# Weight sums for short product units, made stages ahead and kept in DRAM

## The chip, the core and the metric

The kernel runs on one core of one Trainium2 chip, as one program. The core has five engines with queues of their own: PE (TensorE, matmul), DVE (VectorE), ACT (ScalarE), POOL (GpSimd) and SP (SyncE, here only an issuer of DMAs). The metric is the device time of one execution in microseconds, lower is better; a run takes several executions and their median counts.

## What is computed

A trunk of two residual layers over 256 tokens of width 2048, all in float32. Each layer has a token mixer (layer 0: neighbourhood attention with 16 heads; layer 1: a gated short convolution) and a gated MLP of width 5632 with a convolution of three taps between up-projection and activation. Cut to what matters:

```python
for i in range(DEPTH):                       # DEPTH = 2
    a = rms_norm(h, mix_norm[i])
    h = h + (neighborhood_attention(a, ...) if i == 0 else short_conv_mixer(a, ...))
    a = rms_norm(h, ffn_norm[i])
    g, u = jnp.split(dwconv_centered(a @ w_up[i], conv_w) + conv_b, 2, axis=-1)
    h = h + (silu(g) * u) @ w_down[i]
return rms_norm(h, final_norm)
```

## The kernel before

**Precision.** Every float32 operand is split in two parts: `hi`, a copy rounded to the matmul's type (ACT), and `lo = raw - hi` (DVE). A product is the sum of three matmuls, hi x hi, hi x lo and lo x hi. Weights are split on the chip each time they are loaded: `prep_to` takes the next entry of a long list `chunks`, loads up to 512 KB into a buffer tagged `raw` (five of them, from SP's queue, L120 or L124) and calls `parts` (L131), which makes the cast on ACT (L139) and the subtraction on DVE (L140) into buffers `hi` and `lo`, six of each.

**Order.** All stages append their work to three lists: `chunks` (weights to load), `items` (pieces of matmul work) and `ends` (how many chunks an item needs). One loop at the end (L790) goes over the items: it prepares the chunks that the item needs, runs the item, then prepares `AHEAD` = 4 chunks more. `after(n, fn)` puts work off by n ticks of this loop. Each engine runs its own instructions in order; waits are set by the framework from what an instruction reads and writes, and a buffer is taken again only when its last reader is done.

**Two kinds of stage.** A `Phase` (query/key, short convolution "SC", up-projection) has the weights as the stationary operand: for each 128 output columns 16 matmuls of 512 columns (L185) and 16 of 256 (L193), two such columns side by side; each result then goes through an evacuation on ACT and DVE (`both`, `conv`, `split` and others). `Values` (attention's value projection) and `Tokens` (attention's output, the mixer's output, the down-projections) have the tokens as the stationary operand and stream the weights, with the matmuls of `product` (L374). A down-projection comes in two halves of 22 K tiles, each after its own half of the up-projection, which leaves its results in 22 tiles tagged `act`.

**Seven products instead of eight.** `Tokens` works on units: two K tiles, both halves of the tokens, and two groups of 512 columns, a 2 x 2 by 2 x 2 block product. A plain unit takes eight products. The units listed in a plan's second entry go through `seven` (L379): a Winograd form with seven products, which needs sums of the four token blocks (`make_forms`, L421, on POOL, split again on ACT and DVE) and sums of the weight blocks. The weight sums are made by `sums` (L143) when the unit's right-hand chunk arrives: four additions on DVE over 128 x 512, then `parts` for three blocks, of 512, 1024 and 1024 columns. Four of the seven products add up in PSUM tiles of their own (`mu`), and after a plan's last such unit `combine` (L405) adds them to `h`.

**Plans.** Each plan has the order of the units for one pair of column groups, the units in short form, and when `combine` is due. In attention's output the short units are 6 and 7, in the mixer's output 1, 3, 5, in the down-projection's first half 1, 3, 5, 7, 9 in both plans, in the second half 1, 3, 5, 7 and 3, 5, 7. The very last four K tiles of the run are done by `finale` (L364), one output block after the other, so that the closing norm can start early.

**Stages in order of time**: four times query/key and values with attention; attention's output; layer 0: up, down, up, down; SC; mixer's output; layer 1: up, down, up, down, closing norm (`last_evac`).

## Time and profile before

| what | value |
|---|---|
| median of 3 runs | 2204.95 us (2203.89 to 2205.58) |
| span of the profiled execution | 2203.5 us |
| DVE busy | 1752.7 us (80%) |
| ACT busy | 1274.6 us (58%) |
| DMA: moved, mean rate | 421.00 MB, 191 GB/s |
| DMA queue of SP, share of the 16 DMA engines | 58.4% |
| DMA queue of ACT | 0.63 MB |
| written to HBM | 2.10 MB |
| granted clock of PE | 0.998 |

The page gives for each engine the time in which it was busy, and its share of the span. The span runs from the first to the last instruction; the time of a run is a little longer than the span, and the profiled execution's own run isn't among the three. Tables by stage give, after the stretch and its length, the busy time of each engine with its number of instructions, then the granted clock, the share of the DMA engines and the rate. A row of a group of instructions has the line in the code, the engine, the operation, what it writes and reads, how often it ran, the total and the mean in ns, and the idle time before it with what ended that. "A <- B: t, n, longest" in a list of waits says that A waited t us for B, n times.

### The profile page before, as it was taken

Reading aid. Unit: us, or ns where it says so; the run is one execution under the profiler, and the core shown is the slowest. Engines: PE = TensorE matmul, PEld = TensorE weight load, DVE = VectorE, ACT = ScalarE, POOL = GpSimd, SP = SyncE. Lnnn points to the kernel's source line nnn. Section 1 sums busy time; section 2 is a strip of 40 time slices with the busy share of each in tenths; the row PEclk is TensorE's granted clock in tenths of the full one; section 3 lists DMA queues with packets and bytes.
Section 4 is the critical chain, followed back from the end, with each engine's and each line's share of the span. In section 5 each row is a group of like instructions: output and inputs, shape, how many; then the busy total and the mean of one; then the engine's idle time right before and its main releaser. Section 6 shows DMA issues by size and latency. Waiting matters only on the chain.

```text
span 2203.5 us, 31950 instructions
## 1 busy us (share of the span) xinstructions
PE 2191.7 (99%) x11776; PEld 1900.1 (86%) x11776; DVE 1752.7 (80%) x2677; ACT 1274.6 (58%) x1900; POOL 71.4 (3%) x115
## 2 busy tenths in 40 slices
PE   9999999999999999999999999999999999999998
PEld 8888888888888888888888888888888888888886
DVE  8777678877788987778876666898777898777887
ACT  7555556665655565565555445566556556665554
POOL 0000000000000000000000000000000000000000
PEclk9999999999999999999999999999999999999999
DMA  7565546555556755555665555565555566555564
GB/s 259 191 198 180 172 150 211 190 191 191 191 172 196 226 200 186 191 190 185 200 196 189 187 191 183 174 224 180 190 187 184 177 212 219 191 191 192 170 203 134
DMA packets 214605, 421.00 MB, mean 191 GB/s; under 512 B 13488, under 2 KB 142640, under 8 KB 214448
## 3 DMA queue, kind: packets, MB, share of 16 engines
q1 hardware_dynamic: 213072, 418.33, 58.4%
q8 instruction: 92, 1.51, 0.3%
q10 hardware_dynamic: 1376, 0.63, 0.1%
q14 instruction: 65, 0.53, 0.1%
HBM read 416.81 MB, written 2.10 MB: 190 GB/s over the span
## 4 chain that ended last, share of the span: by engine, by line
PE 96%; DVE 1%; DMA 1%; ACT 1%; issue 0%; SPq 0%; DVEq 0%; ACTq 0%
PE mm L185 41%; PE mm L193 22%; PE mm L375 8%; PE mm L376 8%; PE mm L377 8%; PE mu L375 2%; PE mu L377 2%; PE mu L376 2%; PE mm L570 1%; PE mm L572 1%; PE mm L571 1%; DMA raw<-in_wqk 1%; PE tr L284 1%; DVE lo L140 0%; PE tr L525 0%
## 5 line engine op out<-in xcount | busy, mean ns | idle before, releaser
L140 DVE TENSOR_TENSOR lo<-raw,hi 128x1024 fp32r<-128x1024 f32 (+1 forms) x836 | 973.1, 1186 | 188.3 <-PE mm L193 123.4
L139 ACT CAST hi<-raw 128x1024 fp32r<-128x1024 f32 (+1 forms) x836 | 845.7, 1019 | 368.9 <-PE mm L377 121.8
L185 PE MATMUL mm<-a,hi 128*128 128x512 f32 x4096 | 961.7, 391 | 0.9 <-ACT hi L139 0.4
L185 PEld LDWEIGHTS mm<-a,hi 128*128 128x128 f32 x4096 | 759.2, 188 | 153.8 <-DVE a L226 2.0
L193 PEld LDWEIGHTS mm<-a,lo 128*128 128x128 f32 x4096 | 512.9, 192 | 11.9
L193 PE MATMUL mm<-a,lo 128*128 128x256 f32 x4096 | 518.0, 283 | 0.0
L375 PE MATMUL mm<-hi,act 128*128 128x512 f32 x696 | 271.4, 390 | 0.0
L376 PE MATMUL mm<-lo,act 128*128 128x512 f32 x696 | 271.1, 389 | 0.0
L377 PE MATMUL mm<-hi,act 128*128 128x512 f32 x696 | 270.8, 389 | 0.0
L238 ACT COPY corr<-mm 128x256 f32<-128x256 f32 x256 | 94.8, 372 | 240.0 <-PE mm L193 240.0
L254 DVE SCALAR_TENSOR_TENSOR conv<-pad,pt,conv 128x256 f32<-128x256 f32 x384 | 184.8, 482 | 43.8 <-ACT conv L252 28.8
L252 ACT ACTIVATE conv<-pad,pt 128x256 f32<-128x256 f32 x176 | 105.6, 601 | 145.8 <-DVE pad L244 145.8
L377 PEld LDWEIGHTS mm<-hi,act 128*128 128x128 f32 x696 | 130.6, 188 | 27.2
L375 PEld LDWEIGHTS mm<-hi,act 128*128 128x128 f32 x696 | 130.7, 188 | 26.8
L376 PEld LDWEIGHTS mm<-lo,act 128*128 128x128 f32 x696 | 130.7, 188 | 26.6
L239 DVE TENSOR_TENSOR corr<-mm,corr 128x256 f32<-128x256 f32 x256 | 106.9, 418 | 2.0 <-ACT corr L238 1.9
L218 DVE TENSOR_TENSOR act<-conv,act 128x256 fp32r<-128x256 f32 x88 | 37.4, 425 | 85.8 <-ACT act L217 85.8
L244 DVE TENSOR_TENSOR pad<-corr,rstd 128x256 f32<-128x256 f32 x176 | 74.0, 421 | 0.1
L139 ACT CAST hi<-t 128x1024 fp32r<-128x1024 f32 x44 | 46.4, 1054 | 39.6 <-DVE t L152 26.5
L140 DVE TENSOR_TENSOR lo<-t,hi 128x1024 fp32r<-128x1024 f32 x44 | 53.8, 1222 | 4.8 <-ACT hi L139 3.7
L149 DVE TENSOR_TENSOR raw<-raw 128x512 f32<-128x512 f32 x44 | 30.4, 690 | 33.2 <-DMA raw<-in_wdown 28.9
L570 PE MATMUL mm<-hi,a 128*128 128x512 f32 x128 | 50.5, 394 | 0.0
(157 smaller groups left out, 1464.0 us busy)
## 6 DMA issues: line engine op xcount, KB each, us to landing
raw<-in_wup SPq DMA_DIRECT2D x352, 512.0 KB, 4.9
raw<-in_wdown SPq DMA_DIRECT2D x176, 512.0 KB, 4.5
raw<-in_wsc SPq DMA_DIRECT2D x96, 512.0 KB, 4.9
raw<-in_wqk SPq DMA_DIRECT2D x56, 512.0 KB, 4.7
raw<-in_wv SPq DMA_DIRECT2D x32, 512.0 KB, 4.5
raw<-in_wo SPq DMA_DIRECT2D x32, 512.0 KB, 4.5
raw<-in_wscout SPq DMA_DIRECT2D x32, 512.0 KB, 4.4
raw<-in_wqk SPq DMA_DIRECT2D x16, 256.0 KB, 5.1
```

The costliest lines, as they stand in the source:

```text
L139: nc.scalar.copy(out=hv, in_=r)
L140: nc.vector.tensor_sub(out=lv, in0=r, in1=hv.bitcast(F32))
L185: nc.tensor.matmul(self.ps[ft], lhsT=prepped[i][0][:, o:o + P], rhs=self.src[k], start=k == 0, stop=False)
L193: nc.tensor.matmul(self.ps[ft][:, S:], lhsT=prepped[i][1][:, o:o + P], rhs=self.src[k][:, :S], start=False, stop=k == self.nk - 1)
L238: nc.scalar.copy(out=corr, in_=ps[:, S:])
L239: nc.vector.tensor_add(out=corr, in0=ps[:, :S], in1=corr)
L244: nc.vector.tensor_mul(out=dst, in0=both(ps), in1=rstd)
L252: nc.scalar.activation(c, x[:, 1:S + 1], AF.Identity, scale=w[1], bias=b)
L254: nc.vector.scalar_tensor_tensor(out=c, in0=x[:, tap:tap + S], scalar=w[tap], in1=c, op0=ALU.mult, op1=ALU.add)
L375: nc.tensor.matmul(ps, lhsT=xh, rhs=wh, start=start, stop=False)
L376: nc.tensor.matmul(ps, lhsT=xh, rhs=wl, start=False, stop=False)
L377: nc.tensor.matmul(ps, lhsT=xl, rhs=wh, start=False, stop=stop)
```

## The change

It has five parts.

1. **More short units.** Plans are written as words: P plain, S short with sums made on arrival as before, D short with sums made earlier. Each of the four plans of a down-projection's two halves has six short units, two S and four D; the mixer's output has one S and three D in each plan, attention's output keeps its two S.
2. **Jobs.** Each D unit is made in two jobs of kind "make", which stand in `chunks` between the weights of `Phase` stages. A job loads two 256 KB pieces from SP's queue into two `act` tiles, adds four times on DVE (128 x 256 each, four chunks later in the list), and stores the two tiles from ACT's queue into a DRAM tile (seven chunks later). 16 jobs stand in the second and third query/key stages, 8, 8, 8 and the last 2 in the four up-projections, 34 in SC, between an eighth and three quarters of a stage's items (from the first item where that eighth is less than one item).
3. **Loading a D unit.** Four chunks: the left block (512 KB), the second K tile of the right one (256 KB) and two kept ones (512 KB each). `seven` takes the sums in the arrangement in which they were kept, and for a D unit does product "21" two places earlier.
4. **Room.** `sums` makes its second pair in the right-hand chunk's own buffer, not in a tile tagged `qk`. A set of token forms takes 6 blocks of a tile instead of 8; the fourth form goes into the part of an `act` tile that a short unit doesn't read, with a split of its own. `corr` has two buffers instead of four (every other one of the first query/key results goes to a tile tagged `g`). The 512-column blocks of the right chunk share one buffer for `hi` and `lo`.
5. **A sixth `raw` buffer.**

```diff
+S_FIRST = (plan("P0 D1 P2 S3 D4 P5 D6 S7 P8 D9 P10", 3), plan("P0 P2 D1 S3 D4 P5 D6 S7 P8 P10 D9", 6))
+S_SECOND = (plan("P0 P2 D1 S3 D4 P5 D6 S7 D8 P9 P10", 1), plan("P0 P2 P5 D1 S3 D4 S7 D6 D8 P9 P10", 1))
+S_OUT = (plan("P0 D1 S2 P3 D4 D5 P6 P7", 1), plan("P0 P3 D1 S2 D4 D5 P6 P7", 1))
+QK_JOBS, UP_JOBS, SC_JOBS = (0, 8, 8, 0), (8, 8, 8, 4), 34
+S_ATT = (plan("P0 P1 P2 S6 P3 S7 P4 P5", 1),) * 2
...
+RAWS = 6
...
     def prep_to(n):
         while len(prepped) < min(n, len(chunks)):
             src, w, kind = chunks[len(prepped)]
-            raw = wp.tile([P, CH * P], F32, name="raw", tag="raw", bufs=5)
+            for due in [x for x in stores if x[0] <= len(prepped)]:
+                stores.remove(due)
+                due[1]()
+            if kind == "make":
+                make(src, w)
+                prepped.append(())
+                continue
+            raw = wp.tile([P, CH * P], F32, name="raw", tag="raw", bufs=RAWS)
...
+            if kind == "kept":
+                nc.sync.dma_start(out=raw, in_=src().rearrange("p h n -> p (h n)"))
...
     def sums(l, r):
...
         add(out=v13[:, :, 1, :], in0=r[:, :, 1, :], in1=r[:, :, 0, :])
-        add(out=v24[:, :, 0, :], in0=v13[:, :, 0, :], in1=r[:, :, 1, :])
-        add(out=v24[:, :, 1, :], in0=v24[:, :, 0, :], in1=l[:, :, 1, :])
-        return parts(r[:, :, 1:2, :]), parts(t13), parts(t24)
+        w22 = parts(r[:, :, 1:2, :])
+        add(out=r[:, :, 1, :], in0=v13[:, :, 0, :], in1=r[:, :, 1, :])
+        add(out=r[:, :, 0, :], in0=r[:, :, 1, :], in1=l[:, :, 1, :])
+        return w22, parts(t13), parts(r)
+
+    def make(job, half):
+        w, g, i = job
+        if half == 0:
+            kept[id(w), g, i] = dp.tile([P, 2, 2, 4 * P], F32, name=f"kept{len(kept)}")
+        dst = kept[id(w), g, i]
+        tiles = [act_tile().bitcast(F32) for _ in range(2)]
+        for n, x in enumerate(tiles):
+            f = 8 * g + 4 * n + 2 * half
+            nc.sync.dma_start(out=x.rearrange("p (f n) -> p f n", f=2),
+                              in_=w[f:f + 2, :, 2 * i * P:(2 * i + 2) * P].rearrange("f p n -> p f n"))
+        l, r = (x.rearrange("p (f k c) -> p k f c", f=2, k=2) for x in tiles)
+
+        def adds():
+            add = nc.vector.tensor_add
+            add(out=l[:, 0], in0=l[:, 0], in1=r[:, 0])
+            add(out=r[:, 0], in0=r[:, 1], in1=r[:, 0])
+            add(out=r[:, 1], in0=l[:, 0], in1=r[:, 1])
+            add(out=l[:, 1], in0=r[:, 1], in1=l[:, 1])
+
+        def store():
+            for n, x in enumerate(tiles):
+                nc.scalar.dma_start(out=dst[:, n, half], in_=x)
+        stores.append((len(prepped) + 4, adds))
+        stores.append((len(prepped) + 7, store))
...
+            made, lo, hi = 0, len(order) // 8, len(order) * 3 // 4
+            for n, (two, ks) in enumerate(order):
...
                 ends.append(len(chunks))
+                while made < min(len(jobs), max(0, -(-len(jobs) * (n + 1 - lo) // (hi - lo)))):
+                    chunks.append((*jobs[made], "make"))
+                    made += 1
...
+                    elif i in kinds:
+                        chunks.append((right[:, :, P:], P, "cols"))
+                        chunks.extend((lambda j=j, key=(id(w), g, i): kept[key][:, j], 2 * P, "kept") for j in range(2))
+                        items.append((self, g, c + 1, k, k, k + 2))
+                        ends.append(c + 4)
...
-            for ps, x, w, j in ((a, raw(0, 0), left, 0), ("11", raw(1, 0), left, 1), ("12", s4, w22, 0),
-                                (e, s1, t13, 0), (f, s3, t13, 1), (b, s2, t24, 0), ("21", raw(1, 1), t24, 1)):
+            if sset[i] == "S":
+                w22, (t1, t3), (t4, t2) = prepped[c][0], *([(y, j) for j in range(2)] for y in prepped[c][1:])
+            else:
+                w22, (t1, t4), (t3, t2) = prepped[c], *([(y, j) for j in range(2)] for y in prepped[c + 1:c + 3])
+            for ps, x, (w, j) in ((a, raw(0, 0), (left, 0)), ("11", raw(1, 0), (left, 1)), ("12", s4, (w22, 0)),
+                                  (e, s1, t1), *((("21", raw(1, 1), t4),) * (sset[i] == "D")), (f, s3, t3), (b, s2, t2),
+                                  *((("21", raw(1, 1), t4),) * (sset[i] == "S"))):
...
+        n = form_at[0] = (form_at[0] + 1) % 6
+        y = tp.tile([P, 6 * P], F32R, name="sf", tag=("sf", "vv", "qk")[n % 3])
+        hi, lo = y[:, :3 * P], y[:, 3 * P:]
+        split_into(hi, lo, v[:, :3].rearrange("p f c -> p (f c)"))
+        spare = place[:, P:2 * P], place[:, 3 * P:]
+        split_into(*spare, v[:, 3])
```

More of the change, by code (lines that the diff above doesn't have):

```diff
@@ L113, in trunk @@
     prepped = []
+    stores = []
     def prep_to(n):
@@ L312, in __init__ @@
             self.halves = halves
-            for g, (order, sset, _) in enumerate(plan):
+            for g, (order, kinds, _) in enumerate(plan):
                 for i in order:
@@ L467, in qk_evac @@
     def qk_evac(f, ps):
-        c = both(ps)
+        c = both(ps, "g" if waiting and len(held) % 2 else "corr")
         if waiting:
@@ L737, in trunk @@
     mlp(0, a1, to_norm(2, a2))
-    Phase(wsc, range(3 * KT), KT, a2, sc_evac, intro=3)
-    Tokens(wscout, KT, yT, to_norm(3, a3), ((range(KT // 2), S_OUT, 1),) * 2, yforms)
+    Phase(wsc, range(3 * KT), KT, a2, sc_evac, intro=3, jobs=take(SC_JOBS))
+    Tokens(wscout, KT, yT, to_norm(3, a3), S_OUT, yforms)
     mlp(1, a3, last_evac())
```

97 lines of the change are left out of this document (59 added, 38 removed).

## The prediction

> **What bounds the kernel now.** I read the page's busy times first, then the waits of PE and of the load queue, the chain, and last the windows by stage (cut where the timeline's matmuls change from L185/L193 to L375-L377).
>
> ```profile
> PE 2191.7 (99%) x11776; PEld 1900.1 (86%) x11776; DVE 1752.7 (80%) x2677; ACT 1274.6 (58%) x1900; POOL 71.4 (3%) x115
> ...
> PE bc L686 <- DVE conv L684: 1.6, 1, 1.6
> PE st L100 <- DVE inv L645: 1.1, 1, 1.1
> ...
> SPq L120 <- DVE lo L140: 1208.3, 512, 8.2
> SPq L124 <- DVE lo L140: 497.0, 198, 12.6
> ...
> 419.71 7.28 PE mm L185 x32
> 427.00 3.83 PE mm L193 x32
> ```
>
> A busy PE need not be a PE at its peak, so the first line alone proves little. The waits prove it: PE's longest is 1.6 us. The load queue sits 1208.3 and 497.0 us behind VectorE's low-part subtraction (L140), which frees load buffers: loads wait for buffers, not PE for loads. In the chain the matmuls stand back to back, 32 of 512 columns in 7.28 us, 0.2275 us each (32 of 256 columns take 3.83 us). PE sets the end in every stage. What takes matmuls away shortens the run as long as nothing else becomes late.
>
> **The change part by part. Matmuls removed.** A unit (two K tiles, 256 tokens, 1024 columns) has eight products, or seven in the short form, each of three 512-column matmuls. Short units before, from the plans: 5+5+4+3 per MLP layer, 3+3 in the mixer's output, 2+2 in attention's, together 44. After: four plans of 6 per layer, 4+4 and 2+2, together 60. Sixteen more, one product less each: 16 x 3 x 0.2275 = **10.9 us of PE time gone**. No matmul is added.
>
> **Sums moved out of the token stages.** 38 of the 60 are "D" units; two jobs each, 76, make their sums earlier. A job loads 2 x 256 KB, makes four 128x256 additions on VectorE and stores 2 x 256 KB from ACT's queue, 1.05 MB in all. The token stage then loads 512 + 256 + 1024 KB, 1.84 MB instead of 1.05.
>
> ```profile
> L140 DVE TENSOR_TENSOR lo<-raw,hi 128x1024 fp32r<-128x1024 f32 x776 | 935.5, 1224 | 184.4 <-PE mm L193 123.4 <-ACT hi L139 52.2 <-issue 5.8
> L140 DVE TENSOR_TENSOR lo<-raw,hi 128x512 fp32r<-128x512 f32 x60 | 41.0, 688 | 3.9 <-ACT hi L139 3.8
> L151 DVE TENSOR_TENSOR t<-raw 128x512 f32<-128x512 f32 x44 | 30.1, 685 | 0.0
> L601 DVE TENSOR_TENSOR pad<-scx 128x256 f32<-128x256 f32 x16 | 6.8, 423 | 0.2
> ...
> 641.80:754.70 112.90, 112.90 (x500) 93.49 (x499) 101.49 (x124) 64.10 (x70) 0.00 (x0) 1.00 0.67 207
> ```
>
> VectorE in a token stage: an in-place ("S") unit costs 4 x 0.685 + 3 x 1.224 + 0.688 = 7.1 us, a D unit 4.36, a plain one 2 x 1.224 = 2.45. The first down-projection (last row) had 10 S and 12 plain, 100 us by this sum against 101.5 measured; with 4 S, 8 D, 10 plain it is 88, some 89 of 111.5 us. VectorE is relieved there. ACT casts 3.5 blocks of 1024 for a short unit and 2 for a plain one, so it gets three blocks more beside 64.1 of 112.9. The transfers grow from 207 GB/s x 112.9 us = 23.4 MB by 8 x 0.79 to 29.7 MB, 266 GB/s. Value taken: nothing.
>
> **The jobs, where they land.** Eight in each of the second and third query/key stages, 26 in the four up-projections, 34 in the short-convolution (SC) stage, spread from an eighth to three quarters of its items (in the query/key stages from the first). Here covers run thin. An SC item of one chunk is 8 x (0.2275 + 0.12) = 2.78 us, so the 34 fall between the 4th and the 21st of 29 items, from 1124.2 to 1293.7 us.
>
> ```profile
> 83.60:121.60 38.00, 38.00 (x233) 34.11 (x232) 24.45 (x41) 21.12 (x36) 1.02 (x1) 1.00 0.49 154
> 776.90:932.40 155.50, 155.50 (x898) 137.72 (x897) 121.83 (x200) 93.33 (x143) 6.83 (x13) 1.00 0.56 190
> 1124.20:1293.70 169.50, 169.50 (x970) 149.33 (x969) 113.83 (x184) 87.54 (x120) 5.55 (x8) 1.00 0.56 187
> 1115.90:1132.60 16.70, 16.70 (x99) 14.37 (x98) 12.95 (x25) 11.47 (x21) 0.00 (x0) 1.00 0.69 221
> 1132.60:1138.20 5.60, 5.60 (x33) 4.85 (x32) 5.60 (x11) 3.83 (x6) 0.00 (x0) 1.00 0.51 162
> ...
> 690.00:695.00 5.00, 5.00 (x24) 4.14 (x23) 3.68 (x4) 3.10 (x3) 0.00 (x0) 1.00 1.08 380
> 1040.00:1050.00 10.00, 10.00 (x46) 8.26 (x45) 9.45 (x11) 6.82 (x7) 0.00 (x0) 1.00 1.04 353
> ...
> L120 SPq DMA_DIRECT2D raw<-in_wsc x96: 327/328/341, 1097.4 to 1361.6; - x96
> ```
>
> After the times stand PE, PEld, DVE, ACT, POOL, the clock, the DMA share and GB/s.
>
> *VectorE.* A job is 4 x 0.423 = 1.69 us. SC: 113.8 + 34 x 1.69 = 171 us of work in 169.5. Up-projection: 121.8 + 13.5 = 135 of 155.5. Query/key: 24.5 + 13.5 = 38 of 38. SC is worst at its front: four short items (14 us) bring eight jobs, 13.5 us, where VectorE already works 12.95 of 16.7 and 5.60 of 5.6. It falls some 10 us behind and regains under 1 us per pair of columns. A pair's low parts are first read after its 32 high matmuls (7.28 us), and two pairs fit in PSUM, so roughly 10 us of lateness is covered. Bounds: 0 (all covered) to 5 us (the front's overhang counted once and half again). I take **+2 us**, near the covered end, since the front overruns its cover by little.
>
> *DMA.* SC needs 187 GB/s x 169.5 = 31.7 MB plus 34 x 1.05 = 35.7, less some six last stores that slip past the window (3.1): 64.2 MB, or 379 GB/s. Before shows 380 over 5 us and 353 over 10 us, at shares above 1. At 353 it takes 182 us, 12 too many; but the first SC load issues at 1097.4, 18.5 us before its stage, and this lead swallows 12. At 380 nothing is late. I take 0 by the 10 us row, the longer one. Query/key: 154 x 38 = 5.9 + 8.4 = 14.3 MB, 40 us at 353 where there are 38: covered.
>
> A rule of the Trainium skill speaks against this change: the page "DMA: Bandwidth & Descriptors", section "Issuing engines are not separate DMA queues", says that transfers started from SP and from ACT run on the same 16 engines and interleave. By it the stores on ACT's queue count in full, as I counted them; if they ran beside the loads, SC would need only 64.2 - 14.7 = 49.5 MB, 292 GB/s, and no DMA rival were left. No row here has bulk stores.
>
> *Queue order.* A job's load waits on SP for two free activation tiles, with the next weights behind it. 22 exist; each job holds two from its load to its store's landing. A store waits on ACT for VectorE's additions, with the casts behind it; it stands three chunks after them, so it should find them done.
>
> ```profile
> 0.73 0.41 ACTq L94 DMA_DIRECT2D pt<-in_par  x1
> out<-a ACTq DMA_DIRECT2D x4, 128.0 KB, 2.3
> L217 ACT CAST sf<-s 128x512 fp32r<-128x512 f32 x21 | 13.0, 621 | 14.8 <-POOL s L431 14.6
> L218 DVE TENSOR_TENSOR sf<-s,sf 128x512 fp32r<-128x512 f32 x21 | 14.5, 693 | 22.8 <-ACT sf L217 22.8
> ```
>
> Issuing a store costs ACT 0.41 us: 68 in SC, 28 us beside 87.5 of 169.5, hidden. Landing (2.3 us for 128 KB) waits on nobody but the next job.
>
> *Forms.* Token forms grow from 23 to 30 sets, the fourth form now split by itself: 7 more sets of 0.62 us on ACT and 0.69 on VectorE, and one short operation more on each for 28 sets, none longer than those: at most some 5 us of either engine per up-projection half, hidden in the slack above.
>
> *Sixth load buffer, start.*
>
> ```profile
> 0.00:83.60 83.60, 80.62 (x446) 69.91 (x447) 69.46 (x126) 57.42 (x128) 8.62 (x13) 1.00 0.76 251
> ```
>
> PE idles 3.0 us in the first 83.6. A sixth buffer can save between -0.5 and 1.5 of it; I take 0, as later stages wait for buffers from the far side.
>
> *The end.* The last short unit used to be followed by a plain unit before the closing block; now (D8) none stands between.
>
> ```profile
> 2172.55 0.69 DVE L411 TENSOR_TENSOR h<-h,s 128x512 f32<-128x512 f32 x1
> 2180.16 0.69 DVE L417 TENSOR_TENSOR h<-h,s 128x512 f32<-128x512 f32 x1
> 2180.40:2193.50 13.10, 13.02 (x63) 9.87 (x61) 8.30 (x26) 6.29 (x17) 0.00 (x0) 1.00 0.11 34
> 2193.46 0.69 DVE L273 TENSOR_TENSOR h<-mm,h 128x512 f32<-128x512 f32 x1 [0.75 <-PE mm L377]
> ```
>
> The combining additions L410-L417 (eight, 0.6 us apart, about 5 us) stood ahead of the closing block; now they fall into it, on top of VectorE's 8.3 us of 13.1. That fits, barely, before the last residual add. Bounds 0 to 3 us; I take **+1**.
>
> **Sum.** 2203.5 (span) - 10.9 + 2 + 1 = 2195.6. The three runs lie 0.4 to 2.1 us above the span, their median 1.45: **2197.0**.
>
> **Rivals.** (1) *Slower: bulk stores and loads together run below what loads alone reach.* The SC window covers 169.5 + 18.5 (lead) us at no loss; PE then starves for 64.2 MB / rate - 188. The gain of some 10 us is used up at 64.2 / 198 = 324 GB/s. At 300 GB/s the loss is 26 us: 2204.95 - 10.9 + 1 + 26 = 2221. For it: no row shows stores. Against it: share 1.0 went with 353 and 380 GB/s. Chance 0.16. (2) *No change: queues and VectorE give the gain back.* In the query/key stages eight jobs want 16 tiles where eight hold probabilities and four to eight hold outputs: SP may wait up to half a stage (25 us against 18.5 of lead, some 6 each), and SC's front may cost 5 instead of 2. Loss 5 to 14 in place of 2: 2200 to 2209. For it: VectorE at 38 of 38 and 171 of 169.5. Against it: after both backlogs comes a stretch without jobs, and PE's own cover is spent only once. Chance 0.19. (3) *The change doesn't shorten PE's part,* because matmuls next to a fuller SBUF run slower: 1% would cost 22 us. At 380 GB/s above, PE was busy all 5 us; I give it under 0.01 and count it with (1).
>
> **How the numbers follow.** Forecast: 0.62, 2192.5 (no losses, start gains 1.5) to 2200.5. Better than that: 0.03. A measurement here tells about 0.2%, 4.4 us, from no change. Faster by more (below 2200.5): 0.65; within: rival (2), 0.19; slower: rival (1), 0.16. The range of 8 in 10 takes the forecast and rival (2): 2192.5 to 2211.
>
> **What would show it.** Right: 2700 instead of 2748 product matmuls at the same 0.2275 us; token stages about 1.4 to 3.4 us shorter per MLP half (two, then five units) and 1.4 in the mixer's output; SC still near 269 us with DVE near 0.95 and over 350 GB/s. Rival (1): PE waiting for ACT's casts behind late loads in SC, DMA share at 1 with fewer GB/s. Rival (2): SP waiting on stores or on L542's tiles, PE waiting in query/key. Wrong altogether: PE idle in the down-projections.

## The result, and the profile after

The changed kernel takes 2234.0 us (median of 4 runs, 2229.19 to 2236.13) against 2205.22 us for the kernel before on the same chip: ratio 1.013, interval 1.0116 to 1.0145. It is 1.3% slower, where the forecast was 2197.0 us and its range ended at 2211. The profiled execution spans 2231.6 us (before 2203.5, forecast 2195.6).

The page's first part, its shares of the chain and three of its rows for transfers:

```profile
PE 2194.1 (98%) x11728; PEld 1893.3 (85%) x11728; DVE 1836.9 (82%) x2960; ACT 1298.0 (58%) x1967; POOL 102.4 (5%) x143
...
PE 80%; DMA 9%; DVE 7%; issue 2%; ACT 1%; SPq 0%; ACTq 0%; POOL 0%; DVEq 0%
...
raw<-in_wup SPq DMA_DIRECT2D x352, 512.0 KB, 5.0
...
kept<-act ACTq DMA_DIRECT2D x152, 256.0 KB, 4.8
...
act<-in_wdown SPq DMA_DIRECT2D x128, 256.0 KB, 6.0
```

PE ran 48 matmuls fewer, as the change meant, and was yet busy 2.4 us longer and idle 37.5 us in all instead of 11.8. A part of the longer busy time is the clock: right after two of PE's long idle stretches (3.35 us at 1089.4 and 2.45 us at 1452.6) the granted clock was 0.50 for 3.4 us (1093.0 to 1096.4 and 1454.8 to 1458.2), which by that clock is an estimated 1.7 us lost each time; in the kernel before, it fell only at the very end, from 2196.7 us on. The chain that ended last is 9% DMA. The last two rows are the jobs' own: their loads land in 6.0 us (median), their stores in 4.8; above them stand the weight loads of the up-projections.

Stage by stage (windows; after each length stand the busy times of PE, PEld, DVE, ACT, POOL, then clock, DMA share and GB/s): the second query/key stage and its values, the second down-projection of layer 0, SC and the mixer's output of before; then the same of after, and with them the first down-projection of layer 0, whose row of before stands in the prediction.

```profile
83.60:134.50 50.90, 50.90 (x312) 45.74 (x311) 35.09 (x61) 28.96 (x51) 2.04 (x2) 1.00 0.52 165
134.50:157.90 23.40, 23.40 (x113) 19.48 (x112) 17.89 (x29) 11.80 (x22) 2.03 (x2) 1.00 0.71 223
...
999.20:1115.90 116.70, 116.70 (x525) 96.86 (x524) 98.33 (x123) 66.92 (x84) 0.00 (x0) 1.00 0.65 203
1115.90:1385.20 269.30, 269.30 (x1555) 238.14 (x1554) 185.25 (x291) 137.85 (x191) 7.59 (x12) 1.00 0.56 186
1385.20:1470.20 85.00, 85.00 (x385) 70.36 (x384) 78.49 (x102) 51.69 (x69) 0.00 (x0) 1.00 0.63 204
```

```profile
81.80:135.10 53.30, 51.37 (x311) 45.80 (x310) 38.53 (x81) 25.07 (x45) 5.50 (x2) 1.00 0.80 270
135.10:162.50 27.40, 24.28 (x112) 19.55 (x111) 23.59 (x40) 15.08 (x28) 5.85 (x2) 1.00 0.82 273
...
652.30:763.80 111.50, 111.50 (x494) 92.34 (x493) 92.51 (x107) 66.80 (x74) 0.00 (x0) 1.00 0.77 251
1008.30:1132.30 124.00, 117.18 (x511) 94.67 (x509) 106.47 (x139) 72.96 (x91) 0.00 (x0) 0.99 0.82 272
1132.30:1410.20 277.90, 272.39 (x1554) 238.94 (x1555) 223.33 (x413) 135.29 (x200) 15.62 (x16) 1.00 0.88 294
1410.20:1499.40 89.20, 86.28 (x378) 69.82 (x377) 79.28 (x102) 54.21 (x72) 0.00 (x0) 0.98 0.79 268
```

PE fills every stage of before to the last tenth. After, it still does so in the first down-projection, which is 1.4 us shorter (two units x 3 x 0.2275 us), but not in the others shown. All stages of after that aren't in the table below kept their length within 0.2 us. Lengths here and below are from stage cuts as in the prediction, in us; "2nd and 3rd QK+V" are the two query/key stages that have jobs, with their values.

| stage | before | forecast | after | no_jobs | no_adds | no_stores | in_order | spread | best_tied |
|---|---|---|---|---|---|---|---|---|---|
| up to the 2nd QK | 83.6 | 83.6 | 81.8 | 82.1 | 82.7 | 82.2 | 82.5 | 81.9 | 82.0 |
| 2nd and 3rd QK+V | 148.1 | 148.1 | 160.6 | 148.1 | 163.9 | 155.4 | 159.6 | 148.1 | 148.1 |
| layer 0, 1st down | 112.9 | 111.5 | 111.5 | 111.5 | 111.5 | 111.5 | 111.5 | 111.5 | 112.9 |
| layer 0, 2nd down | 116.7 | 113.3 | 124.0 | 116.8 | 125.1 | 119.7 | 116.8 | 115.6 | 116.5 |
| SC | 269.3 | 271.3 | 278.0 | 269.3 | 269.4 | 281.7 | 286.6 | 269.3 | 269.0 |
| mixer's output | 85.0 | 83.6 | 89.2 | 83.6 | 88.0 | 86.4 | 84.0 | 83.6 | 85.0 |
| layer 1, 1st down | 112.9 | 111.5 | 111.5 | 111.5 | 111.5 | 111.5 | 111.5 | 111.5 | 111.5 |
| layer 1, 2nd down | 129.0 | 126.6 | 129.3 | 129.9 | 129.9 | 130.5 | 129.7 | 126.4 | 127.0 |
| span | 2203.5 | 2195.6 | 2231.6 | 2198.9 | 2227.9 | 2224.7 | 2229.1 | 2194.0 | 2198.2 |

The spans of the changed kernel's four runs lie between 2227.4 and 2234.3 us, and the table has one trace of each kernel. So a difference of a few us between two losing stages may be the spread between runs; stages at PE's pace repeat within some 0.4 us.

Against the forecast the span lost 36.0 us: 12.5 in the query/key stages, 10.7 in layer 0's second down-projection, 6.7 in SC, 5.6 in the mixer's output, 2.7 in the last stage, less some 2 won elsewhere, 1.8 of it at the start.

**The wait that the forecast's sum didn't hold.** VectorE's waits for jobs' loads, and PE's two longest waits, after ("A <- B: us in total, times, longest"):

```profile
DVE act L204 <- DMA act<-in_wdown: 34.2, 19, 5.6
...
DVE act L204 <- DMA act<-in_wscout: 11.4, 4, 5.6
```

```profile
PE mu L455 <- DVE lo L172: 5.7, 6, 3.4
PE mm L267 <- DVE lo L172: 5.3, 9, 1.9
```

L204 is a job's first addition. VectorE stood 45.6 us before it because the job's load hadn't landed; the subtractions (L172) queued behind it then kept PE waiting. Here is one place in SC where VectorE stood, from VectorE's timeline (start, length, what, and in brackets the idle time before it):

```profile
1179.65 0.43 DVE L204 TENSOR_TENSOR act<-act 128x256 f32<-128x256 f32 x1 [5.60 <-DMA act<-in_wscout]
1179.99 1.22 DVE L172 TENSOR_TENSOR lo<-raw,hi 128x1024 fp32r<-128x1024 f32 x1
```

Behind this one PE waited only 0.55 us for a subtraction (at 1189.89); behind a stand of 3.31 us before 1277.60 it waited 1.87 us.

Over the whole of SC VectorE's waits for jobs' loads come to 24.3 us (the list of waits, cut to that stage):

```profile
DVE act L204 <- DMA act<-in_wdown: 17.9, 7, 5.6
DVE act L204 <- DMA act<-in_wscout: 6.4, 2, 5.6
```

The loss doesn't come at SC's front, where the prediction looked for it. These are its first 129.7 us and the next 60 us (columns as above):

```profile
1132.30:1262.00 129.70, 129.15 (x742) 114.06 (x743) 106.44 (x209) 63.96 (x98) 6.67 (x8) 1.00 0.93 308
1262.00:1322.00 60.00, 55.04 (x306) 46.84 (x305) 47.26 (x90) 24.05 (x35) 1.65 (x1) 1.00 0.96 334
```

In the first stretch VectorE stood 14.7 us for loads and PE was idle for 0.55 us; in the second it stood 9.0 us more and PE was idle for 4.96 us. In in_order (below), with all 34 jobs in SC, PE was busy for the whole of SC's first 70 us. So the cover for VectorE's lateness seems to have lasted for the 18 jobs of the first stretch and to have been used up then.

And one place in the second query/key stage, from the chain (start, length, what) and from ACT's timeline:

```profile
124.90 7.97 DMA act<-in_wdown
...
132.96 0.42 DVE act L204
133.39 0.34 DVE act L206
133.72 1.16 DVE act L205
```

```profile
129.87 0.40 ACT L291 CAST qk<-qk 128x256 fp32r<-128x256 f32 x1
133.76 2.31 ACTq L211 DMA_DIRECT2D kept<-act  x3
136.11 0.37 ACT L312 COPY corr<-mm 128x256 f32<-128x256 f32 x1 [5.84 <-DMA kept<-act]
```

The job's load took 7.97 us to land, the additions came at once behind it, and ACT did nothing from 130.27 to 133.76 because the next thing in its queue was a store that waited for an addition. Three stores then took 2.31 us to issue, and an evacuation (L312) came after 5.84 us without work on ACT. The bracket names the store's transfer; what held ACT is the store standing ahead of the copy, which the ACTq row between them shows. The Trainium skill, page "DMA: Bandwidth & Descriptors", section "Anatomy of one DMA — SWDGE (gpsimd) path", says (of another issuing path) that a transfer's semaphore wait is spent on the issuing sequencer, not in the DMA engines; these 3.49 us on ACT's queue agree.

**Where the jobs ran.** VectorE's time in L204, by stage (window, length, busy time and count of that line, then clock, DMA share, GB/s): the second down-projection of layer 0, SC and the mixer's output.

```profile
1008.30:1132.30 124.00, 2.02 (x5) 0.99 0.82 272
1132.30:1410.20 277.90, 12.01 (x29) 1.00 0.88 294
1410.20:1499.40 89.20, 0.84 (x2) 0.98 0.79 268
```

SC's list has 34 jobs, and it ran 29. The first five ran in the token stage before it, one whole stage ahead; two meant for layer 1's first up-projection ran in the mixer's output. These two token stages were not to hold any jobs, and both lost time. (Two more ran in attention's output, which lost none.)

### The profile page after: what moved, and what is told of

Read it like the earlier page. It is cut to its first block, busy times and chain, and to the rows that moved or that the text cites. A ratio compares the mean times of both kernels' runs of the same rounds, so it can differ in the third digit from the quotient of the medians.

```text
span 2231.6 us, 33123 instructions
## 1 busy us (share of the span) xinstructions
PE 2194.1 (98%) x11728; PEld 1893.3 (85%) x11728; DVE 1836.9 (82%) x2960; ACT 1298.0 (58%) x1967; POOL 102.4 (5%) x143
## 4 chain that ended last, share of the span: by engine, by line
PE 80%; DMA 9%; DVE 7%; issue 2%; ACT 1%; SPq 0%; ACTq 0%; POOL 0%; DVEq 0%
PE mm L259 36%; PE mm L267 19%; PE mm L454 5%; PE mm L455 5%; PE mm L456 5%; DMA act<-in_wdown 3%; DVE lo L172 3%; DMA raw<-in_wsc 2%; PE mu L454 2%; PE mu L456 2%; PE mu L455 2%; DMA raw<-in_wdown 1%; PE mm L660 1%; PE mm L662 1%; PE mm L661 1%
## 5 line engine op out<-in xcount | busy, mean ns | idle before, releaser
L171 ACT CAST hi<-raw 128x1024 fp32r<-128x1024 f32 (+1 forms) x912 | 908.9, 1013 | 390.6 <-PE mm L456 94.2
L172 DVE TENSOR_TENSOR lo<-raw,hi 128x1024 fp32r<-128x1024 f32 (+1 forms) x852 | 1013.0, 1209 | 128.3 <-ACT hi L171 71.8
L454 PE MATMUL mm<-hi,act 128*128 128x512 f32 x656 | 256.8, 392 | 2.6 <-DVE h L347 2.5
L456 PE MATMUL mm<-hi,act 128*128 128x512 f32 x656 | 256.0, 390 | 0.0
L455 PE MATMUL mm<-lo,act 128*128 128x512 f32 x600 | 234.4, 391 | 1.3 <-DVE lo L172 1.3
L312 ACT COPY corr<-mm 128x256 f32<-128x256 f32 x256 | 93.9, 371 | 228.1 <-PE mm L267 182.3
L454 PEld LDWEIGHTS mm<-hi,act 128*128 128x128 f32 x656 | 123.7, 189 | 29.1 <-issue 2.8
L456 PEld LDWEIGHTS mm<-hi,act 128*128 128x128 f32 x656 | 123.5, 188 | 25.8
L455 PEld LDWEIGHTS mm<-lo,act 128*128 128x128 f32 x600 | 113.3, 189 | 25.6 <-DVE lo L172 2.5
L455 PE MATMUL mu<-lo,sf 128*128 128x512 f32 x168 | 67.0, 399 | 5.8 <-DVE lo L172 5.7
L204 DVE TENSOR_TENSOR act<-act 128x256 f32<-128x256 f32 x76 | 31.4, 420 | 45.9 <-DMA act<-in_wdown 34.2
L454 PE MATMUL mu<-hi,sf 128*128 128x512 f32 x168 | 66.0, 393 | 0.3 <-ACT hi L171 0.3
L456 PE MATMUL mu<-hi,sf 128*128 128x512 f32 x168 | 66.1, 394 | 0.0
```

The source lines that it names most:

```text
L171: nc.scalar.copy(out=hv, in_=r)
L172: nc.vector.tensor_sub(out=lv, in0=r, in1=hv.bitcast(F32))
L312: nc.scalar.copy(out=corr, in_=ps[:, S:])
L454: nc.tensor.matmul(ps, lhsT=xh, rhs=wh, start=start, stop=False)
L455: nc.tensor.matmul(ps, lhsT=xh, rhs=wl, start=False, stop=False)
L456: nc.tensor.matmul(ps, lhsT=xl, rhs=wh, start=False, stop=stop)
```

## The experiments

Line numbers move by up to four in the kernels with longer edits. "Before" had a median of 2204.65 to 2205.43 us in each set. Where no ratio is given, a time is that of a single run; a span is that of the profiled execution.

**no_jobs.** No jobs are made; D units load other weights in place of the kept sums, so what they add to `h` isn't the layer's product.

```diff
-        out, jobs[:] = jobs[:n], jobs[n:]
-        return out
+        return []
...
-(lambda j=j, key=(id(w), g, i): kept[key][:, j], 2 * P, "kept")
+(lambda j=j, i=i: wup[j, i, :, :CH * P].rearrange("p (h n) -> p h n", h=2), 2 * P, "kept")
```

> The changed kernel without any job: no early loads, additions or stores; a D unit loads two 512 KB blocks of another weight in place of the kept sums, so its output isn't the reference's, but every matmul, split and token-stage load stays. The changed kernel's span is 2231.6 us. Every theory that blames the jobs (waits for their loads, their additions as work, their transfers) expects a span of 2193 to 2197: 2203.5 less 10.9 plus 0 to 4 for the closing block and the dense second down-projection. A theory that blames the D units' own larger loads in the token stages expects the second down-projection and the mixer's output to stay 5 to 15 us too long in sum: 2205 to 2215.

2200.64 us. Query/key, SC and the mixer's output run at PE's pace (table). So the jobs are 33 us of the loss (2231.6 - 2198.9). What is left without them is 3.5 us over the forecast in layer 0's second down-projection and 3.3 in layer 1's.

**no_adds.** The additions are left out, loads and stores stay; the kept data aren't sums.

```diff
-        stores.append((len(prepped) + 4, adds))
```

> Jobs load and store, but VectorE's four additions are left out (the kept blocks are then plain weights, not the reference's). Theory 'wait' (VectorE stands in its queue until a job's load lands, 45.6 us in the changed kernel's trace, and all behind it is late): VectorE can't be blocked any more, only ACT's stores can; span 2197 to 2210. Theory 'work' (the 127 us of additions overfill VectorE): 2195 to 2205. Theory 'traffic' (80 MB of job transfers delay the weights): 2225 to 2232.

2229.64 us. SC, with its windows row:

```profile
1137.60:1407.00 269.40, 269.31 (x1556) 238.25 (x1555) 185.75 (x295) 133.83 (x200) 13.34 (x16) 1.00 0.88 302
```

All of the traffic, at 302 GB/s through the stage, and PE is busy from end to end: bulk stores beside loads don't slow SC. Its loss needs the additions. The span is yet only 3.7 us shorter than in the change, because the query/key stages lose 3.3 us more and two other stages some. The query/key stages and layer 0's second down-projection stay slow without them: now the stores wait for the loads themselves, and ACT with them:

```profile
ACT corr L311 <- DMA act<-in_wdown: 37.2, 14, 5.2
```

**adds_apart.** Five additions of 128x96 per job on a tile of their own that nobody reads, in place of the four on the job's tiles; the kept data aren't sums.

```diff
-            add(out=l[:, 0], in0=l[:, 0], in1=r[:, 0])
...
+            for _ in range(5):
+                add(out=apart, in0=apart, in1=apart)
```

> As the run without additions, but VectorE does five additions of 128x96 per job on a small tile of its own (some 1.5 us, about the 1.7 of the four left out), at the same place in the list and depending on no load; kept blocks are plain weights. Theory 'wait': about as without additions, at most 5 us longer, 2197 to 2213. Theory 'work': like the changed kernel, 2225 to 2232. Theory 'traffic': 2225 to 2232.

2244.21 us. It was to keep VectorE's work and take away its wait for the load, and doesn't tell these apart, for the work moved. All instructions of that line:

```profile
L206 DVE TENSOR_TENSOR lead<-lead x380: 227/258/1078, 1.0 to 355.8; 128x96 f32<-128x96 f32 x190
```

The list spreads them over the whole run, and the last started at 355.8 us. SC had none (270.4 us), the query/key stages, full of them, took 168.8. It shows that the framework, which writes each engine's order, puts an instruction where its operands allow and not where the list has it.

**no_stores.** Loads and additions stay, the stores go; D units load other weights.

```diff
-        stores.append((len(prepped) + 7, store))
```

> Jobs load and add, but store nothing, and D units load other weights in place of kept sums (output not the reference's). Activation tiles come free earlier, ACT issues no stores, 40 MB less move. Theory 'wait' on loads alone: VectorE still waits for loads, though tiles come free sooner, so loads start earlier: 2210 to 2225. Theory 'traffic': stores are half of it, 2205 to 2215. Theory 'work': 2225 to 2232.

2226.47 us. The query/key stages lose 7.2 us in place of 12.5, SC more than in the change (12.4 in place of 8.7). So in SC it isn't ACT standing in front of stores that costs, for here it has none to issue. Beside no_adds, which keeps loads and stores and loses nothing there, this leaves the additions: their work, or VectorE's wait for the loads. That wait is as it was, 45.5 us in all, most of it here:

```profile
DVE act L204 <- DMA act<-in_wdown: 36.6, 20, 5.1
```

**up_jobs.** The jobs of query/key and all but six of SC's go to the up-projections, some 16 in each.

```diff
-QK_JOBS, UP_JOBS, SC_JOBS = (0, 8, 8, 0), (8, 8, 8, 4), 34
+QK_JOBS, UP_JOBS, SC_JOBS = (0, 0, 0, 0), (16, 22, 16, 16), 6
```

> The changed kernel with the jobs moved: none in query/key, 16, 22, 16 and 16 in the four up-projections, 6 in the short-convolution stage. Theory 'wait' (a job costs where tiles are scarce, so that its load comes only 6 to 8 us before the additions, in front of urgent casts; in the up-projections jobs cost nothing): query/key and values give back their 12.4 us, SC and the mixer's output at least 10 of 13, the second down-projection 0 to 7; span 2200 to 2209 instead of 2231.6. Rival 'each job costs the same wherever it stands' (some 0.4 us of VectorE and DMA): 2225 to 2232, with the up-projections some 15 us longer in sum.

2243.72 us, ratio 1.0178 (1.0163 to 1.0193): worse. Query/key and SC are back, but the four up-projections, untouched at up to eight jobs, lose 6.7, 6.0, 5.9 and 4.0 us, and the token stages behind them up to 6.2. PE's longest wait is now for ACT's casts (L171, 13.0 us in 16 times, all in the up-projections), not for subtractions. VectorE waits 81.9 us for jobs' loads:

```profile
DVE act L204 <- DMA act<-in_wdown: 59.9, 38, 2.9
DVE act L204 <- DMA act<-in_wscout: 22.0, 8, 4.6
```

**in_order.** Additions are tied behind the low-part subtraction that stands before them in the list, stores behind the cast.

```diff
-        nc.scalar.copy(out=hv, in_=r)
-        nc.vector.tensor_sub(out=lv, in0=r, in1=hv.bitcast(F32))
+        last_cast[:] = [nc.scalar.copy(out=hv, in_=r), nc.vector.tensor_sub(out=lv, in0=r, in1=hv.bitcast(F32))]
...
+            with tc.issue_after(last_cast[1].ins):
                 add(out=l[:, 0], in0=l[:, 0], in1=r[:, 0])
...
+                with tc.issue_after(last_cast[0].ins):
                     nc.scalar.dma_start(out=dst[:, n, half], in_=x)
```

> The changed kernel, but a job's additions and stores are issued behind the cast and the subtraction of the chunk that stands before them in the list, so that they can't move ahead on VectorE and ACT. Theory 'moved ahead' (the framework's scheduler pulls a job's work to the earliest place at which it believes the load to be there, ahead of casts that PE needs sooner): VectorE's waits for job loads fall from 45.6 us to under 10, the second down-projection, SC and the mixer's output give back most of 20 us: 2208 to 2218. Rival 'traffic or latency alone': waits and span stay, 2227 to 2235. Tiles are held longer, so query/key may get up to 10 us worse under either.

2230.88 us. The two token stages, with L206 (here a job's first addition), and SC between them:

```profile
1008.00:1124.80 116.80, 0.00 (x0) 1.00 0.80 270
1124.80:1411.40 286.60, 14.07 (x34) 0.99 0.86 293
1411.40:1495.40 84.00, 0.00 (x0) 1.00 0.80 271
```

No addition runs ahead, and the token stages are 7.1 and 5.2 us shorter, 12.3 together: moving ahead is the cause there. SC, now with all 34, loses 17.3 in place of 8.7 and takes most of it back, so the span is only 2.5 us shorter, and the time lies among the changed kernel's runs. VectorE's waits for jobs' loads hardly fall, to 40.2 us, where the theory expected under 10: a late load isn't the work of moving ahead alone.

**spread.** As no_jobs, and one plan of the second halves is spread out, to see what is left of the loss without jobs.

```diff
-plan("P0 P2 P5 D1 S3 D4 S7 D6 D8 P9 P10", 1)
+plan("P0 D1 S3 D4 P2 D6 S7 D8 P5 P9 P10", 1)
```

> As the run without jobs (span 2198.9; output not the reference's), but the second half's second plan reads P0 D1 S3 D4 P2 D6 S7 D8 P5 P9 P10: plain units between the short ones, and one before the closing block. Theory 'density' (four D and two S units in a row ask VectorE for 31.6 us of work in 28.7 us of PE, and the combining falls into the closing block): the second down-projection 113.3 to 114 us instead of 116.8, the last stage 126 to 127 instead of 129.9: 2192 to 2195. Rival 'the D units' larger loads cost that, wherever they stand': 2197 to 2200.

2195.82 us, span 2194.0, 4.9 below no_jobs. The second down-projections win 1.1 and 2.6 us against before, in place of losing 0.1 and 0.9; 3.4 each was to come from the matmuls.

**up_spread** is up_jobs with that plan.

> Jobs moved as in the run with jobs in the up-projections, and the second plan spread as in the run before this one; complete and meant to be faster than both kernels. Theories 'wait' and 'density' together: 2192 to 2201 span. If six jobs left in SC still cost dearly: 2202 to 2207. Rival 'same cost everywhere': above 2220.

2242.26 us, ratio 1.0174 (1.0157 to 1.0191). With 16 jobs per up-projection that plan makes no difference.

**early.** Weights of a phase are kept behind the last job's load on SP, so that this load comes well before its additions. **up_early** has the edits of up_spread too, **few_early** those of few (below).

```diff
             if kind == "rows":
-                nc.sync.dma_start(out=raw[:, :w], in_=src)
+                with ExitStack() as behind:
+                    if job_load:
+                        behind.enter_context(tc.issue_after(job_load[0].ins))
+                    nc.sync.dma_start(out=raw[:, :w], in_=src)
...
-            nc.sync.dma_start(out=x.rearrange("p (f n) -> p f n", f=2),
+            job_load[:] = [nc.sync.dma_start(out=x.rearrange("p (f n) -> p f n", f=2),
```

> The changed kernel with the weight loads that follow a job in the list kept behind the job's own loads on SP; in the changed kernel's order on SP, 8 to 12 later weight loads had been put ahead of most of them. Theory 'late loads' (additions stand where they should, but their loads are issued 6 to 8 us before them, no more than they take to land): VectorE's waits for job loads fall from 45.6 us to under 10; SC comes back to 269 to 272; the first five jobs still run in the second down-projection, which stays near 120 to 124; 2210 to 2222. Rival 'work and traffic': SC stays above 275, 2228 to 2236. In query/key SP may now stand for tiles: up to 5 us either way.

> Jobs in the up-projections and the spread plan (2240.8 us span as it was), with the job loads in their place on SP. Theory 'late loads': the up-projections' 27 us in sum come back almost wholly, VectorE's waits for job loads fall from 83 us to under 15: span 2205 to 2216, the rest being jobs that still run in token stages. Rival 'work' (16 to 22 jobs overfill VectorE in an up-projection: 196 + 22 x 1.7 = 234 of 244.5 us): up-projections stay 3 us or more too long each, span above 2228.

2574.16 us, and 2811.36 (ratio 1.2751, 1.2734 to 1.2768). VectorE's waits for jobs' loads fall to 9.8 and 1.6 us, and PE starves instead, some 7 us at a time. PE's longest wait in early:

```profile
PE mm L263 <- ACT hi L175: 247.9, 35, 9.5
```

**few.** 32 jobs, eight in each up-projection, none in query/key or SC; the down-projections have more S units, the mixer's output is as before.

```diff
-S_FIRST = (plan("P0 D1 P2 S3 D4 P5 D6 S7 P8 D9 P10", 3), ...
-S_SECOND = (plan("P0 P2 D1 S3 D4 P5 D6 S7 D8 P9 P10", 1), ...
+S_FIRST = (plan("P0 S1 P2 S3 D4 P5 S6 D7 P8 S9 P10", 3), plan("P0 P2 S1 P5 S3 D4 P8 S6 D7 P10 S9", 6))
+S_SECOND = (plan("P0 P2 S1 S3 D4 P5 S6 D7 P8 P9 P10", 1), plan("P0 S1 P2 S3 D4 P5 D7 S6 P8 P9 P10", 1))
+S_OUT = (plan("P0 S1 P2 S3 P4 S5 P6 P7", 1),) * 2
+QK_JOBS, UP_JOBS, SC_JOBS = (0, 0, 0, 0), (8, 8, 8, 8), 0
```

> Only as many jobs as cost nothing in the changed kernel: 8 in each up-projection, none elsewhere. Six short units per plan in the first halves (2 D, 4 S), five in the second (2 D, 3 S), mixer's output as before: 54 short units instead of 44, 10 x 0.6825 = 6.8 us less PE time. Theory 'a job costs only where VectorE has no slack for its work and its wait': all stages at PE's pace, span 2194 to 2199, faster than both kernels. Rival 'every job costs': 32 x 0.4 = 13 us, span above 2206.

> The run with few jobs, with the job loads in their place on SP. Where jobs cost nothing before, the order of loads can give nothing: within 2 us of the run with few jobs. If late loads cost there too, up to 4 us less.

few takes 2206.3 us, ratio 1.0007 (0.9999 to 1.0016): the same as before, not the span of 2194 to 2199 that was expected. Its up-projections run at PE's pace, the second halves win 1.25 and 2.0 us, but the first halves, with four S in each plan, lose 2.4 and 2.9. VectorE waits 8.2 us for jobs' loads in the whole run. few_early takes 2492.01 us (ratio 1.1301, 1.1286 to 1.1317). Its chain, around one job in the first up-projection:

```profile
489.32 1.93 PE mm L271 x16
...
491.68 0.43 DVE corr L317
...
497.73 0.43 DVE act L208
...
499.10 0.44 DVE act L211
499.54 1.04 ACT hi L175
...
500.62 2.50 PE mm L263 x5
```

PE's last matmuls end, their evacuation runs on VectorE (L317 and on), then the job's additions (L208 to L211), and only then ACT casts the next weights (L175), which PE has waited for. The casts stand on ACT behind the job's store, the store waits for the additions, and these stand on VectorE behind the evacuation of the very item that PE was running: a ring through three queues. PE waits for such casts 28 times, 219.7 us in all, with 32 jobs.

**few_own** and **few_own_early.** As few and few_early, but a job's tiles are a pair of its own, and the load buffers are five.

```diff
-        tiles = [act_tile().bitcast(F32) for _ in range(2)]
+        tiles = [wp.tile([P, 2 * S], F32, name="job", tag="job", bufs=2) for _ in range(2)]
...
-RAWS = 6
+RAWS = 5
```

> As few, but the jobs' two tiles are a pair of their own (256 KB each) instead of spare activation tiles; to make room the load buffers go back from six to five. Theory (the activation tiles make the job's load late): the load is issued at once when its turn comes, the additions no longer wait for it (in few VectorE waited 8.2 us for jobs' loads and each load was issued about 6 us ahead of its additions), and the time is that of few or a little less: 2202 to 2206. Rival (the queue makes it late, whatever the tile: the load stands behind weight loads that wait for load buffers): still about 6 us ahead, VectorE still waits about 8 us, and five buffers instead of six cost what the sixth gave at the start, some 1.5 us: 2206 to 2210.

> As few_own, and weight loads of a phase are kept behind the last job's load on SP's queue, as in few_early (2492). Theory (the activation tile was what the queue waited for there): with tiles of their own the job's load is never held, so the queue isn't, the loss of some 290 us vanishes and the time is 2202 to 2212. Rival (the tie itself breaks the lead of the weights, by the place it gives to the job's load): it stays above 2400.

2253.85 and 2251.22 us. The first is far from both expectations: freed from the activation tiles, the jobs meant for the up-projections ran from 55 us on, at the rate at which two tiles let them, through query/key, values and attention's output. These lost 8.4, 6.4, 2.7 and 12.7 us, and none was left after 680 us:

```profile
680.00:1200.00 520.00, 0.00 (x0) 1.00 0.62 205
```

So the activation tiles, handed out in the list's order, are what kept the jobs near their place. They aren't the only thing that makes a load late: in the stages where the jobs now ran, additions still came 3 to 9 us behind its issue (once 15), and VectorE waited 31.9 us for it, more than in few:

```profile
DVE job L204 <- DMA job<-in_wdown: 31.9, 12, 3.7
```

That the loss of few_early is gone in few_own_early says little, because there were no jobs left in the up-projections for its ring. Why the load and the additions of a job end up so close together stays open.

**best**, from the stages measured so far: sums in the stage, as before, in layer 0's first down-projection and the mixer's output; layer 1's first one as in the change; the second ones as in few. 32 jobs: none, 8, 8, 8 in the up-projections, 8 in SC.

```diff
+S_FIRST = ((plan("P0 S1 P2 S3 P4 S5 P6 S7 P8 S9 P10", 3), plan("P0 P2 S1 P4 S3 P6 S5 P8 S7 P10 S9", 6)),
+           (plan("P0 D1 P2 S3 D4 P5 D6 S7 P8 D9 P10", 3), plan("P0 P2 D1 S3 D4 P5 D6 S7 P8 P10 D9", 6)))
...
+QK_JOBS, UP_JOBS, SC_JOBS = (0, 0, 0, 0), (0, 8, 8, 8), 8
```

> Layer 0's first down-projection, attention's output and the mixer's output as before (all sums in the stage, five and three units); layer 1's first down-projection as in the change (four in the stage and eight ahead of it, 16 jobs: 8 in SC, 8 in the up-projection before it); both second down-projections as in few (four in the stage, four ahead, 8 jobs in the up-projection before each). From the stages measured so far: start -1.4, first half of layer 1 -1.36, second halves -1.25 and -2.0, jobs 0 at eight per stage: span 2203.5 - 6.0 = 2197.5, time about 2199, ratio 0.997. Rival (jobs cost about 0.4 us each wherever they are, hidden so far in the noise of the stages): 32 x 0.4 = 13 less the gain of 6: 2210, ratio 1.002. Second rival (the gains of the stages depend on the plan before them and don't add): within 2 us of before, 2203 to 2206.

2201.39 us, ratio 0.9983 (0.9974 to 0.9992). It is 2.7 us of span over the expected 2197.5, all in layer 0's second down-projection (118.3), where two of SC's jobs ran ahead. **best_tied** adds the ties of in_order, **best_no_sc** has layer 1's first down-projection as before and no jobs in SC:

> best, with the ties of in_order (additions behind the low-part subtraction before them in the list, stores behind the cast before them). Theory (the two jobs moved ahead cost layer 0's second down-projection 2.8 us): that stage back from 118.3 to about 115.5, SC still 269 to 271 with eight jobs, time 2198.5 to 2200.5, ratio about 0.9975. Rival (the ties delay the subtractions or casts of SC and the up-projections, as they cost 8.6 us in SC with 34 jobs): stage back, but 1 to 2 us lost in each of the stages with jobs: 2202 to 2207.

> best, with layer 1's first down-projection as before (all sums in the stage) and so only 16 jobs, eight in the up-projection before each second down-projection. Theory: nothing is moved ahead into layer 0's second down-projection (115.5), layer 1's first one takes 112.9 instead of 111.55: best's 2201.4 - 2.8 + 1.4 = 2200.0, ratio 0.9977. Rival (the stage's 118.3 comes from its plan beside six load buffers, not from the moved jobs): 2201.4 + 1.4 = 2202.8.

2198.84 us, ratio 0.9973 (0.9964 to 0.9983), and 2200.54 us, 0.9981 (0.9972 to 0.999). That stage is 116.5 and 115.4 us long: the jobs moved ahead were the cause again, and the tie takes back 1.8 of the 2.8 us. In the mixer's output, which has no D units here, two jobs that ran ahead in best had cost nothing (85.0). best_tied is 0.27% faster than before. Its SC, with eight jobs, is at PE's pace, and layer 1's second down-projection takes the 127.0 us of few:

```profile
1114.10:1383.10 269.00, 269.00 (x1555) 238.17 (x1555) 197.01 (x326) 137.09 (x194) 6.11 (x12) 1.00 0.66 214
...
2071.20:2198.20 127.00, 118.06 (x536) 96.87 (x534) 106.99 (x155) 71.09 (x101) 0.00 (x0) 0.97 0.61 195
```

VectorE still stands before the loads of those jobs, in SC alone 19.0 us for eight, and PE loses nothing by it (list of waits, cut to SC):

```profile
DVE act L206 <- DMA act<-in_wdown: 19.0, 6, 4.0
```

## Why the prediction was wrong, point by point

**Matmuls removed: right.** 11776 became 11728. Where nothing else came in, the stages shortened by what was forecast: 1.36 us in both first down-projections, 1.35 in the mixer's output of no_jobs. Without jobs and with one plan spread the span is 2194.0, below the forecast of 2195.6.

**"VectorE: a job is 4 x 0.423 = 1.69 us": the term that failed.** The work was right (L204 measures 0.42 us), but the time that VectorE stands before the first addition was no part of the sum. In the change it is 45.6 us over 76 jobs, 0.6 us each; in SC alone 24.3. Put into the prediction's own sum for SC's 169.5 us, with the jobs that ran there: 113.8 + 29 x 1.69 + 24.3 = 187.1, 17.6 too many; less the 10 us that the prediction held for covered, 7.6, where 8.7 were lost. in_order: 113.8 + 34 x 1.69 + 25.1 = 196.4, 16.9 lost by this sum and 17.3 measured. no_stores: 113.8 + 29 x 1.69 + 28.3 = 191.1, 11.6 and 12.4. Without the waits the three sums are 162.8, 171.3 and 162.8 and lose nothing. best_tied, with eight jobs in SC: 113.8 + 8 x 1.69 + 19.0 = 146.3, no loss by the sum and none measured. That the wait and not the work made the difference is worked out, not shown by itself: no run kept the additions' work in SC and took their wait away. The 10 us of cover are the prediction's own estimate. In the up-projections of up_jobs the same sum passes 155.5 us too (121.8 + 14 x 1.69 + 18.1 = 163.6 in the first), but 6.7 us are lost where 10 were to be covered, and PE's waits there are for ACT's casts. So the sum fits SC, and in the up-projections it leaves something out that no run separates.

**"A store waits on ACT for VectorE's additions ... so it should find them done": wrong.** "Three chunks after them" holds in the list, and each engine's queue was not in the list's order. The additions stood right behind their load's landing, mostly 6 to 10 us after its issue, and the stores 2 to 5 us behind them; so ACT stood too. In the query/key stages this and the tiles held by the jobs cost 12.5 us: none of it goes when only the additions go, 5.2 when the stores go, all when the jobs go. How the other 7.2 divide between waiting loads and scarce tiles wasn't separated.

**"The jobs, where they land": wrong for nine jobs of 76, and dear.** They ran a stage early, seven of them in token stages that were to gain. in_order shows that these two stages lost 12.3 us by it, a third of the whole error. Not all of this was to be had: with these jobs back in SC, SC loses 8.6 us more.

**Token stages "relieved": half right.** The first halves gained what they should. The second halves fell 3.5 and 3.3 us short of the forecast even without jobs. Spreading the units gave 1.2 and 3.5 us back; what the rest of the first is, stays open. The spread plan has fewer short units in a row and also one plain unit before the closing block, so it doesn't tell which of the two cost it, the density or the combining additions close to the end.

**DMA at 0: right.** SC moved 294 GB/s on the average, with 10 us at 371. The second row is no_adds, the 169.5 us from 8.3 us into SC on, the stretch for which the prediction made its sum:

```profile
1270.00:1280.00 10.00, 9.06 (x48) 7.63 (x46) 4.92 (x9) 4.51 (x5) 0.00 (x0) 1.00 1.01 371
...
1145.90:1315.40 169.50, 169.50 (x972) 149.81 (x971) 110.78 (x177) 78.26 (x116) 6.04 (x9) 1.00 0.97 337
```

That is rival (1)'s stage. Loads and stores together kept 337 GB/s through the whole stretch, above its deciding 324, and PE was busy all the time. So the result lay on that rival's side of zero, by another mechanism. Of the page weighed there, "DMA: Bandwidth & Descriptors" of the Trainium skill, section "Issuing engines are not separate DMA queues", the runs show that it holds: without the stores SC's DMA share fell from 0.88 to 0.70 and its rate from 294 to 235 GB/s.

**Rival (2) named the stages, not the size.** Query/key and SC's front were to cost 5 to 14 us together; query/key and SC cost 21.1 (SC not at its front), and the two token stages another 11.5 against before.

**Sixth load buffer, start: better than taken.** 1.8 us won up to the second query/key stage, where 0 was taken and 1.5 was the bound; in the other kernels of the table it is 0.9 to 1.7. No run has the sixth buffer as its only change, so how much of this is the buffer's stays open.

## What to carry to other kernels

Work moved beside other work on in-order engines is priced by its duration and by how long its queue stands before it: a load that lands after its first reader's turn has come holds all that is queued behind the reader. Ask of each moved step what its operands allow, because that, and not its place in a list, sets where it runs; what holds it there (a buffer, a tie) has to be named. And move only as much as leaves the engine's stage slack with the waits counted: eight jobs per up-projection were free, 14 to 22 cost 4 to 7 us.

## What the runs showed of the hardware that wasn't expected

Reads and bulk writes together reached 371 GB/s over 10 us with a DMA share of 1.01, as fast as the loads alone of before (353 over 10 us). A job's load of 256 KB took no less time to land (6.0 us, median) than a weight load of 512 KB (5.0 in the up-projections, 5.9 in SC).
